# RWKV time mixing on one core: whole batches a tile, a fixed order of instructions over 512-token units, float32 stores from the sync queue

## The chip, the cores and the metric

The kernel runs on one core of a Trainium2 chip. A time is the device time of one execution in microseconds (us). Each kernel below was run four to six times, beside runs of the kernel before on the same chip; all runs were of the fast state, with a mean granted TensorE clock between 0.98 and 1.00. A ratio compares one kernel's runs with the runs of the kernel before in the same rounds; it isn't quite the ratio of the medians quoted beside it. The times of a profile are counted from the start of its span; a span is about 2 us shorter than the time.

The engines are called PE (matmuls; PEld is its weight load), DVE (VectorE), ACT (ScalarE), POOL (GpSimd) and SP (the sync queue), as the profile names them.

## The reference

```python
batch, seq_len, d_model = (16, 2048, 256)
x_prev[:, 1:, :] = x[:, :-1, :]              # the token before; zero for the first of a batch
xv = x * time_mix_v + x_prev * (1 - time_mix_v)
xr = x * time_mix_r + x_prev * (1 - time_mix_r)
v = xv @ value_weight
r = xr @ receptance_weight
out = (sigmoid(r) * v) @ output_weight       # float32; the key branch does not reach the output
```

x and out are 33.5 MB each. The kernels fold `time_mix` into the weights, so that what is left per element is `mix = c * x_prev + x` with `c = 1/time_mix - 1`, for v and for r.

## The kernel before

A tile is 1024 consecutive tokens; half of it, 512 tokens, is called a unit here. There are 64 units. The instruction order is left to the compiler's scheduler.

```python
for b in range(B):
    for it in range(NT):                                  # 2 tiles a batch
        nc.gpsimd.dma_start(out=x_bf, in_=x[b, t0:t0+T, :].rearrange("(tb p) d -> p tb d", p=P))
        # 16 transposes on PE into two PSUM tiles, then
        nc.scalar.copy(out=xt[:, :, 1:1+TH], in_=psum_xt[0])
        nc.scalar.copy(out=xt[:, :, 1+TH:1+T], in_=psum_xt[1])
        nc.vector.tensor_copy(out=xt[:, :, 0:1], in_=prev_xt[:, :, T:T+1])
        # mix: four scales of 1024 elements, two adds of 2048, all on DVE
        ...
        for h in range(2):                                # a unit
            # psum_v: 4 matmuls, psum_r: 4 matmuls (512 columns each)
            nc.scalar.activation(out=s_sb, in_=psum_r, func=ACT.Sigmoid)
            nc.vector.tensor_tensor(out=z_sb, in0=s_sb, in1=psum_v, op=ALU.mult)
            # psum_o: 8 matmuls of 256 columns on z_sb
            nc.scalar.copy(out=o_sb[:, h], in_=psum_o)    # o_sb is bf16
        nc.gpsimd.dma_start(out=out[...], in_=o_sb)       # casts to float32 on the way
```

In PSUM, the memory that matmuls write, the kernel keeps two buffers for transposes and one each for v, r and the output.

Of the kernel before, what the change touches and what calls it, by code (L numbers as in the profile page):

```python
# [1 line left out]

# [6 lines left out]
FP32 = mybir.dt.float32  # L10
BF16 = mybir.dt.bfloat16
ALU = mybir.AluOpType
ACT = mybir.ActivationFunctionType


@with_exitstack
def kernel(
    ctx: ExitStack,
    tc: tile.TileContext,
    x: bass.AP,  # L20
    time_mix_k: bass.AP,
    time_mix_v: bass.AP,
    time_mix_r: bass.AP,
    key_weight: bass.AP,
    value_weight: bass.AP,
    receptance_weight: bass.AP,
    output_weight: bass.AP,
    out: bass.AP,
):
    nc = tc.nc  # L30

    B, S, D = x.shape
    P = 128
    KO = D // P
    TH = 512
    T = 2 * TH
    HB = TH // P
    NT = S // T
    XTW = T + 8

    consts = ctx.enter_context(tc.tile_pool(name="consts", bufs=1))

    ident = consts.tile([P, P], BF16)
    make_identity(nc, ident)

    tmv_sb = consts.tile([P, KO], FP32)
    nc.sync.dma_start(out=tmv_sb, in_=time_mix_v.rearrange("(ko p) -> p ko", p=P))
    tmr_sb = consts.tile([P, KO], FP32)
    nc.sync.dma_start(out=tmr_sb, in_=time_mix_r.rearrange("(ko p) -> p ko", p=P))

    cv_sb = consts.tile([P, KO], FP32)
    nc.vector.reciprocal(cv_sb, tmv_sb)
    nc.vector.tensor_scalar(  # L53
        out=cv_sb, in0=cv_sb, scalar1=-1.0, scalar2=None, op0=ALU.add
    )
    cr_sb = consts.tile([P, KO], FP32)
    nc.vector.reciprocal(cr_sb, tmr_sb)
    nc.vector.tensor_scalar(
        out=cr_sb, in0=cr_sb, scalar1=-1.0, scalar2=None, op0=ALU.add
    )  # L60
    c_sb = [cv_sb, cr_sb]

    ones = consts.tile([P, T], BF16)
    nc.vector.memset(ones, 1.0)
    c_full = []
    for m in range(2):
        cf = consts.tile([P, KO, T], BF16, name=f"c_full{m}")
        for ko in range(KO):
            nc.scalar.mul(out=cf[:, ko, :], in_=ones, mul=c_sb[m][:, ko : ko + 1])  # L69
        c_full.append(cf)  # L70

    wv_f32 = consts.tile([P, KO, D], FP32)
    nc.sync.dma_start(out=wv_f32, in_=value_weight.rearrange("(ko p) n -> p ko n", p=P))
    wr_f32 = consts.tile([P, KO, D], FP32)
    nc.sync.dma_start(
        out=wr_f32, in_=receptance_weight.rearrange("(ko p) n -> p ko n", p=P)
    )

    wv_bf = consts.tile([P, KO, D], BF16)
    wr_bf = consts.tile([P, KO, D], BF16)  # L80
    wo_bf = consts.tile([P, KO, D], BF16)
    for ko in range(KO):
        nc.scalar.mul(out=wv_bf[:, ko, :], in_=wv_f32[:, ko, :], mul=tmv_sb[:, ko : ko + 1])
        nc.scalar.mul(out=wr_bf[:, ko, :], in_=wr_f32[:, ko, :], mul=tmr_sb[:, ko : ko + 1])
    nc.gpsimd.dma_start(out=wo_bf, in_=output_weight.rearrange("(ko p) n -> p ko n", p=P))  # L85

    xpool = ctx.enter_context(tc.tile_pool(name="xpool", bufs=4))
    xtpool = ctx.enter_context(tc.tile_pool(name="xtpool", bufs=3))
    mixpool = ctx.enter_context(tc.tile_pool(name="mixpool", bufs=3))
    zpool = ctx.enter_context(tc.tile_pool(name="zpool", bufs=4))  # L90
    opool = ctx.enter_context(tc.tile_pool(name="opool", bufs=3))
    ps_xt_pool = ctx.enter_context(tc.tile_pool(name="ps_xt", bufs=2, space=bass.MemoryType.PSUM))
    ps_vr_pool = ctx.enter_context(tc.tile_pool(name="ps_vr", bufs=1, space=bass.MemoryType.PSUM))
    ps_o_pool = ctx.enter_context(tc.tile_pool(name="ps_o", bufs=1, space=bass.MemoryType.PSUM))

    prev_xt = None
    for b in range(B):
        for it in range(NT):
            t0 = it * T

            x_bf = xpool.tile([P, 2 * HB, D], BF16, name="x_bf")
            nc.gpsimd.dma_start(  # L102
                out=x_bf,
                in_=x[b, t0 : t0 + T, :].rearrange("(tb p) d -> p tb d", p=P),
            )

            xt = xtpool.tile([P, KO, XTW], BF16, name="xt")

            psum_xt = []
            for h in range(2):  # L110
                ps = ps_xt_pool.tile([P, KO, TH], BF16, name="ps_xt")
                for tb in range(HB):
                    for ko in range(KO):
                        nc.tensor.transpose(  # L114
                            out=ps[:, ko, tb * P : (tb + 1) * P],
                            in_=x_bf[:, h * HB + tb, ko * P : (ko + 1) * P],
                            identity=ident,
                        )
                psum_xt.append(ps)
            nc.scalar.copy(out=xt[:, :, 1 : 1 + TH], in_=psum_xt[0])  # L120
            nc.scalar.copy(out=xt[:, :, 1 + TH : 1 + T], in_=psum_xt[1])  # L121

            if it == 0:
                nc.vector.memset(xt[:, :, 0:1], 0.0)
            else:
                nc.vector.tensor_copy(out=xt[:, :, 0:1], in_=prev_xt[:, :, T : T + 1])  # L126
            prev_xt = xt

            mix = mixpool.tile([P, 2, KO, T], BF16, name="mix")
            for m in range(2):  # L130
                for ko in range(KO):
                    nc.vector.tensor_scalar(  # L132
                        out=mix[:, m, ko, :],
                        in0=xt[:, ko, 0:T],
                        scalar1=c_sb[m][:, ko : ko + 1],
                        scalar2=None,
                        op0=ALU.mult,
                    )
            xwin = xt[:, :, 1 : T + 1]
            for m in range(2):  # L140
                nc.vector.tensor_tensor(  # L141
                    out=mix[:, m], in0=mix[:, m], in1=xwin, op=ALU.add
                )

            o_sb = opool.tile([P, 2, HB, D], BF16, name="o_sb")
            for h in range(2):
                psum_v = ps_vr_pool.tile([P, KO, TH], FP32, name="psum_v")
                psum_r = ps_vr_pool.tile([P, KO, TH], FP32, name="psum_r")
                for mo in range(KO):
                    for ko in range(KO):  # L150
                        nc.tensor.matmul(  # L151
                            out=psum_v[:, mo, :],
                            lhsT=wv_bf[:, ko, mo * P : (mo + 1) * P],
                            rhs=mix[:, 0, ko, h * TH : (h + 1) * TH],
                            start=(ko == 0),
                            stop=(ko == KO - 1),
                        )
                for mo in range(KO):
                    for ko in range(KO):
                        nc.tensor.matmul(  # L160
                            out=psum_r[:, mo, :],
                            lhsT=wr_bf[:, ko, mo * P : (mo + 1) * P],
                            rhs=mix[:, 1, ko, h * TH : (h + 1) * TH],
                            start=(ko == 0),
                            stop=(ko == KO - 1),
                        )

                s_sb = zpool.tile([P, KO, TH], BF16, name="s_sb")
                nc.scalar.activation(out=s_sb, in_=psum_r, func=ACT.Sigmoid)  # L169
                z_sb = zpool.tile([P, KO, TH], BF16, name="z_sb")  # L170
                nc.vector.tensor_tensor(out=z_sb, in0=s_sb, in1=psum_v, op=ALU.mult)  # L171

                psum_o = ps_o_pool.tile([P, HB, D], FP32, name="psum_o")
                for j in range(HB):
                    for ko in range(KO):
                        nc.tensor.matmul(  # L176
                            out=psum_o[:, j, :],
                            lhsT=z_sb[:, ko, j :: HB],
                            rhs=wo_bf[:, ko, :],
                            start=(ko == 0),  # L180
                            stop=(ko == KO - 1),
                        )
                nc.scalar.copy(out=o_sb[:, h], in_=psum_o)  # L183

            nc.gpsimd.dma_start(  # L185
                out=out[b, t0 : t0 + T, :].rearrange("(h p j) d -> p h j d", p=P, j=HB),
                in_=o_sb,
            )


# [28 lines left out]
```

## Time and profile before

| | before |
|---|---|
| time, median of the first three runs | 261.0 us (259.3 to 261.8) |
| span of the profiled run | 258.6 us |
| busy share PE / DVE / ACT | 81 / 79 / 74% |
| a unit in the steady part | 3.58 us |
| first v or r matmul, start of the last z | 17.5 us, 249.3 us |

### The profile page before, as it was taken

Reading aid. Unit: us, or ns where it says so; the run is one execution under the profiler, and the core shown is the slowest. Engines: PE = TensorE matmul, PEld = TensorE weight load, DVE = VectorE, ACT = ScalarE, POOL = GpSimd, SP = SyncE. Lnnn points to the kernel's source line nnn. Section 1 sums busy time; section 2 is a strip of 40 time slices with the busy share of each in tenths; the row PEclk is TensorE's granted clock in tenths of the full one; section 3 lists DMA queues with packets and bytes.
Section 4 is the critical chain, followed back from the end, with each engine's and each line's share of the span. In section 5 each row is a group of like instructions: output and inputs, shape, how many; then the busy total and the mean of one; then the engine's idle time right before and its main releaser. Section 6 shows DMA issues by size and latency. Waiting matters only on the chain.

```text
span 258.6 us, 3915 instructions
## 1 busy us (share of the span) xinstructions
PE 208.8 (81%) x1508; PEld 136.5 (53%) x1536; DVE 205.3 (79%) x293; ACT 192.0 (74%) x202; POOL 53.0 (20%) x71
## 2 busy tenths in 40 slices
PE   0288989888988889888889888988888987787860
PEld 0265655555666556565556655655555664354430
DVE  3087999888889888888888998888888899885330
ACT  6678979777777887877777788787777777645640
POOL 7031421222222211222222221112211111100111
PEclk9999999999999999999999999999999999999997
DMA  5999999999999999999999999999974343344444
GB/s 114 188 198 197 150 270 220 275 230 233 227 202 200 197 214 245 238 219 231 228 230 213 197 195 206 243 243 224 224 205 162 111 153 119 116 153 165 162 162 162
DMA packets 43362, 51.24 MB, mean 198 GB/s; under 512 B 1616, under 2 KB 35152, under 8 KB 43344
## 3 DMA queue, kind: packets, MB, share of 16 engines
q0 software_dynamic: 42256, 50.47, 89.3%
q1 hardware_dynamic: 1088, 0.53, 0.7%
q8 instruction: 12, 0.20, 0.3%
q14 instruction: 6, 0.05, 0.1%
HBM read 34.34 MB, written 33.55 MB: 263 GB/s over the span
## 4 chain that ended last, share of the span: by engine, by line
issue 67%; POOL 16%; PE 6%; DMA 4%; ACT 3%; POOLq 1%
POOL x_bf L102 8%; POOL out_dram L185 8%; DMA x_bf<-in_x_dram 4%; PE ps_xt L114 2%; PE psum_v L151 2%; PE psum_r L160 1%; PE psum_o L176 1%; ACT xt L120 1%; ACT s_sb L169 1%; ACT xt L121 1%; POOL wo_bf L85 0%; ACT o_sb L183 0%; POOLq L214 0%; POOLq L185 0%; POOLq L102 0%
## 5 line engine op out<-in xcount | busy, mean ns | idle before, releaser
L171 DVE TENSOR_TENSOR z_sb<-s_sb,psum_v 128x1024 bf16<-128x1024 bf16 x64 | 77.8, 1216 | 31.6 <-PE psum_v L151 28.3
L183 ACT CAST o_sb<-psum_o 128x1024 bf16<-128x1024 f32 x64 | 65.9, 1030 | 37.3 <-PE psum_o L176 37.3
L176 PE MATMUL psum_o<-wo_bf,z_sb 128*128 128x256 bf16 x512 | 67.3, 274 | 16.5 <-DVE z_sb L171 16.4
L169 ACT ACTIVATE s_sb<-psum_r 128x1024 bf16<-128x1024 f32 x64 | 66.0, 1032 | 17.5 <-PE psum_r L160 16.6
L141 DVE TENSOR_TENSOR mix<-mix,xt 128x2048 bf16<-128x2048 bf16 x64 | 77.7, 1218 | 0.0
L160 PE MATMUL psum_r<-mix,wr_bf 128*128 128x512 bf16 x244 | 65.2, 379 | 5.1 <-ACT s_sb L169 4.4
L176 PEld LDWEIGHTS <-z_sb 128*128 128x128 bf16 x512 | 52.1, 115 | 30.8 <-DVE z_sb L171 30.5
L151 PE MATMUL psum_v<-mix,wv_bf 128*128 128x512 bf16 x240 | 64.3, 382 | 0.7 <-issue 0.2
L114 PE MATMUL ps_xt<-ident,x_bf 128*128 128x128 bf16 x512 | 41.0, 228 | 20.5 <-DMA x_bf<-in_x_dram 12.0
L185 POOL DMA_DIRECT2D out_dram<-o_sb x32 | 22.6, 705 | 169.2 <-ACT o_sb L183 169.2
L114 PEld LDWEIGHTS <-x_bf 128*128 128x128 bf16 x512 | 35.6, 102 | 37.8 <-issue 15.4
L160 PEld LDWEIGHTS <-wr_bf 128*128 128x128 bf16 x256 | 25.1, 98 | 30.1 <-issue 0.7
L132 DVE TENSOR_SCALAR mix<-xt,cv_sb 128x1024 bf16<-128x1024 bf16 x64 | 28.7, 490 | 9.4 <-ACT xt L121 9.3
L120 ACT COPY xt<-ps_xt 128x1024 bf16<-128x1024 bf16 x32 | 32.7, 1021 | 3.7 <-PE ps_xt L114 3.7
L102 POOL DMA_DIRECT2D x_bf<-in_x_dram x32 | 29.0, 907 | 30.5 <-PE ps_xt L114 30.4
L151 PEld LDWEIGHTS <-wv_bf 128*128 128x128 bf16 x256 | 25.2, 99 | 16.1 <-issue 0.6
L121 ACT COPY xt<-ps_xt 128x1024 bf16<-128x1024 bf16 x32 | 33.1, 1034 | 0.0
L132 DVE TENSOR_SCALAR mix<-xt,cr_sb 128x1024 bf16<-128x1024 bf16 x64 | 28.5, 484 | 0.0
L126 DVE COPY xt<-xt 128x2 bf16<-128x2 bf16 x16 | 2.7, 169 | 1.2
L69 ACT ACTIVATE c_full<-ones,cv_sb 128x1024 bf16<-128x1024 bf16 x2 | 2.2, 1140 | 1.4 <-DVE cv_sb L53 1.4
L69 ACT ACTIVATE c_full<-ones,cr_sb 128x1024 bf16<-128x1024 bf16 x2 | 2.2, 1132 | 0.0
L69 ACT ACT_TABLE_LOAD x1 | 1.3, 1283 | 0.7 <-PEq L203 0.7
(16 smaller groups left out, 8.0 us busy)
## 6 DMA issues: line engine op xcount, KB each, us to landing
out_dram<-o_sb POOLq DMA_DIRECT2D x32, 1024.0 KB, 4.9
x_bf<-in_x_dram POOLq DMA_DIRECT2D x32, 512.0 KB, 7.2
wv_f<-in_value_weight_dram SPq DMA_DIRECT2D x1, 256.0 KB, 4.2
wr_f<-n_receptance_weight_dram SPq DMA_DIRECT2D x1, 256.0 KB, 4.3
wo_bf<-in_output_weight_dram POOLq DMA_DIRECT2D x1, 128.0 KB, 4.5
tmv_sb<-in_time_mix_v_dram SPq DMA_DIRECT2D x1, 1.0 KB, 2.1
tmr_sb<-in_time_mix_r_dram SPq DMA_DIRECT2D x1, 1.0 KB, 2.2
```

The lines of the kernel that those rows point to most:

```text
L102: nc.gpsimd.dma_start(out=x_bf, in_=x[b, t0 : t0 + T, :].rearrange("(tb p) d -> p tb d", p=P),)
L114: nc.tensor.transpose(out=ps[:, ko, tb * P : (tb + 1) * P], in_=x_bf[:, h * HB + tb, ko * P : (ko + 1) * P], identity=ident,)
L121: nc.scalar.copy(out=xt[:, :, 1 + TH : 1 + T], in_=psum_xt[1])
L132: nc.vector.tensor_scalar(out=mix[:, m, ko, :], in0=xt[:, ko, 0:T], scalar1=c_sb[m][:, ko : ko + 1], scalar2=None, op0=ALU.mult,)
L141: nc.vector.tensor_tensor(out=mix[:, m], in0=mix[:, m], in1=xwin, op=ALU.add)
L151: nc.tensor.matmul(out=psum_v[:, mo, :], lhsT=wv_bf[:, ko, mo * P : (mo + 1) * P], rhs=mix[:, 0, ko, h * TH : (h + 1) * TH], start=(ko == ...
L160: nc.tensor.matmul(out=psum_r[:, mo, :], lhsT=wr_bf[:, ko, mo * P : (mo + 1) * P], rhs=mix[:, 1, ko, h * TH : (h + 1) * TH], start=(ko == ...
L169: nc.scalar.activation(out=s_sb, in_=psum_r, func=ACT.Sigmoid)
L171: nc.vector.tensor_tensor(out=z_sb, in0=s_sb, in1=psum_v, op=ALU.mult)
L176: nc.tensor.matmul(out=psum_o[:, j, :], lhsT=z_sb[:, ko, j :: HB], rhs=wo_bf[:, ko, :], start=(ko == 0), stop=(ko == KO - 1),)
L183: nc.scalar.copy(out=o_sb[:, h], in_=psum_o)
L185: nc.gpsimd.dma_start(out=out[b, t0 : t0 + T, :].rearrange("(h p j) d -> p h j d", p=P, j=HB), in_=o_sb,)
```

## The change

The intent is to let PE and DVE run without waiting for each other, and to move data in long runs. Its parts:

1. **Layout.** One batch (2048 tokens) is a tile; token p*16+j lies in partition p, so that a partition's data is one run of 16 KB in HBM. After the transposes, a block of 128 columns holds the tokens of one j, and the previous token is in the block before; only block 0 needs a shifted copy of block 15, one a batch.
2. **Order.** `manual_schedule()` fixes the order of the program. For each unit PE does r, v, a group of eight transposes seven units ahead, and the output projection of the unit before.
3. **Stores.** The output tile is float32 and goes out from the sync queue, 1 MB at a time, in place of a bf16 tile cast by a GpSimd DMA.
4. **Start.** The first batch is loaded in pieces, unneeded constants are gone, and a ramp does more transposes and mix pieces a turn than the steady part.

```diff
+    ctx.enter_context(tc.manual_schedule())
-                in_=x[b, t0 : t0 + T, :].rearrange("(tb p) d -> p tb d", p=P),
+        src = x[b].rearrange("(p j) d -> p j d", p=P)
 ...
+        nc.scalar.copy(out=xt[b][:, :, c0 : c0 + TU], in_=ps)          # in transposes(g)
+        if e == UB - 1 and b > 0:
+            nc.vector.tensor_copy(
+                out=xt[b][:, :, 1:P], in_=xt[b][:, :, J * P : (J + 1) * P - 1]
+            )
 ...
+            o_sb[b] = opool.tile([P, J, D], FP32, name="o_sb")
+            nc.sync.dma_start(out=dst[:, a : a + 2 * UJ, :], in_=o_sb[b][:, a : a + 2 * UJ, :])
 ...
+    for g in range(NU):
+        ps_r = project(g, 0, ps_r_pool, "psum_r")
+        nc.scalar.activation(out=s_sb, in_=ps_r, func=ACT.Sigmoid)
+        ps_v = project(g, 1, ps_v_pool, "psum_v")
+        took = take_pieces(g + 3, 1 if g > 8 else 2)      # mix pieces: (half batch, v or r)
+        for piece in took:
+            mixing_scale(*piece)
+        nc.vector.tensor_tensor(out=z_sb, in0=s_sb, in1=ps_v, op=ALU.mult)
+        for piece in took:
+            mixing_add(*piece)
+        advance(START_T[g] if g < len(START_T) else g + LOOK)   # START_T = [3, 4, 7, 9], LOOK = 7
+        if z_prev is not None:
+            output(g - 1, z_prev)
+        z_prev = z_sb
+    output(NU - 1, z_prev)
```

## The prediction

> **What bounds the kernel now.** I read the page first (busy shares, slices, costliest groups), then the list of waits, then one stretch of the timeline in the steady part, last the table of stretches. The shares:
>
> ```profile
> PE 208.8 (81%) x1508; PEld 136.5 (53%) x1536; DVE 205.3 (79%) x293; ACT 192.0 (74%) x202; POOL 53.0 (20%) x71
> ...
> PE   0288989888988889888889888988888987787860
> DMA  5999999999999999999999999999974343344444
> ```
>
> Three engines stand at 74 to 81%, none is full, and no slice of PE stays at 9: this is a kernel bound by waits between nearly balanced engines. The DMA row at 9 looks like a bound and has to be ruled out. The list of waits does that, as the only waits of PE for a transfer are three at the start:
>
> ```profile
> PEld L176 <- DVE z_sb L171: 30.5, 38, 1.9
> DVE z_sb L171 <- PE psum_v L151: 28.3, 29, 2.1
> PE psum_o L176 <- DVE z_sb L171: 16.4, 33, 1.4
> PE ps_xt L114 <- DMA x_bf<-in_x_dram: 12.0, 3, 10.4
> PE ps_xt L114 <- ACT xt L120: 8.1, 24, 0.5
> ```
>
> The first and third lines are one loop: PE's output projection waits for VectorE's product z, and z waits (second line) for PE's v projection of the same 512 tokens. Each engine waits for the other in turn. The timeline of one tile (1024 tokens, two units of 512) shows it:
>
> ```profile
> 63.31 1.22 DVE L171 TENSOR_TENSOR z_sb<-s_sb,psum_v 128x1024 bf16<-128x1024 bf16 x1 [0.82 <-PE psum_v L151]
> 64.36 0.44 PE L114 MATMUL ps_xt<-ident,x_bf 128*128 128x128 bf16 x5 [0.29 <-ACT xt L120]
> 64.64 1.04 PE L176 MATMUL psum_o<-wo_bf,z_sb 128*128 128x256 bf16 x8
> 65.51 0.38 PE L151 MATMUL psum_v<-mix,wv_bf 128*128 128x512 bf16 x1
> ...
> 67.37 0.70 POOL L185 DMA_DIRECT2D out_dram<-o_sb  x1 [4.90 <-ACT o_sb L183]
> 68.44 1.06 PE L176 MATMUL psum_o<-wo_bf,z_sb 128*128 128x256 bf16 x8 [0.43 <-DVE z_sb L171]
> ...
> 74.52 0.71 POOL L185 DMA_DIRECT2D out_dram<-o_sb  x1 [5.30 <-ACT o_sb L183]
> ```
>
> The two stores lie 7.15 us apart: that is a tile, so 3.58 us a unit. In brackets are the waits: 0.82 us of VectorE and 0.43 plus 0.29 of PE in each tile.
>
> **What the Trainium skill says.** "TensorE: Matmul & The Clock Gate", Back-to-back issue gap, gives about 216 ns for an isolated 512-column matmul and about 81 ns for a 128-column one with its weight load. The trace: four projection matmuls from 64.64 plus 0.87 to the next group, 0.87/4 = 217 ns, which agrees; a transpose with its load took about 68 ns (16 loads in 1.09 us), a little less than the page. "VectorE: DVE Perf Modes", The perf-mode tier table: a two-tensor operation reaches 2x at most on bf16 in SBUF and 1x with a PSUM operand. The trace agrees: 1218 ns for 2048 elements, the same 1216 ns for 1024 with PSUM. Neither shape is changed. "SBUF — State Buffer", Who interferes with whom: VectorE in a two-port mode and GpSimd block one another, and GpSimd writes the descriptors of its own DMAs. It shows once here: a scale pair that began at 30.99 took 1.19 us instead of 0.88 beside a load issue at 30.85 that took 1.10 instead of 0.90. "DMA: Bandwidth & Descriptors", Issuing engines are not separate DMA queues: moving the stores to the sync queue saves only issue time. No run here shows that yet.
>
> **The change part by part.**
>
> Removed: the unused constant tiles (4 ScalarE operations, 2.19 + 2.17 us at the start), the descriptor work of 32 stores on GpSimd (22.6 us, off the path), half of its load issues (32 to 16, plus the pieces of the first batch).
>
> Not removed: the arithmetic of a unit. I take the distance from start to start in back-to-back stretches, which is the real cost of an instruction in a full engine.
> - PE: r 0.87, v 0.87, output 0.87 (64.64 to 65.51), eight transposes 8 x 0.068 = 0.55. Sum 3.16 us.
> - VectorE: z 1.13 (67.17 to 68.30), add 1.13, two scales 0.80 (65.24 to 66.04 for the pair). Sum 3.06. Added: one shift copy of 2x127 elements per batch; the two-element copy took 0.17, I estimate 0.3 us, over four units 0.08. Sum 3.14.
> - ScalarE: sigmoid, transposed x, output at about 0.92 from start to start. Sum 2.8. Float32 instead of bf16 output shouldn't matter: the cast and the bf16 copy cost the same now (1030 and 1021 ns).
>
> Moved: the order. Output of unit g-1 is issued after the v projection of g, so PE no longer waits for a z in progress; transposes run seven units ahead; mix is made at least one unit ahead. With r(g) starting at 0: r results at 1.03, v at 1.90, transposes end 2.4, output 3.35. Sigmoid starts 1.12 to 1.22 and ends by 2.25; z starts 2.31, ends 3.52. The next v needs z's PSUM banks at 3.16 + 0.87 = 4.03, so 0.5 us are spare. VectorE after z: add at 3.45, scales at 4.58, free at 5.38; the next z is due at 2.31 + 3.16 = 5.47, spare 0.09. ScalarE's output copy starts at 3.45 and leaves the next sigmoid at most 0.1 late. So the loop closes at PE's 3.16 us, and VectorE (3.14) is nearly the same. Steady gain: 3.58 - 3.16 = 0.42 us a unit.
>
> Start: now the first tile's load lands at 10.44, the first v matmul begins at 17.46. Changed: the first 4-row piece is 0.5 MB instead of 1 MB. Successive tiles landed at 10.44, 13.14 and 15.78, so about 1 MB of float32 per 2.65 us, 0.4 MB/us. Half a megabyte less is 1.3 us, and it leads the queue: I estimate 7 us. Cold transposes 0.9, ScalarE copy 1.0, four half-size scales 1.1, one half-size add 0.7: first r matmul at about 11. The ramp is not free. Units 2 to 5 need their mix before VectorE has caught up, and up to unit 6 PE does 13 groups of transposes and VectorE 9 pieces of mix; stepping the orders of both through by hand gives r(6) at 35 us instead of 11 + 6 x 3.16 = 30. Some of it is work done early (about six groups of transposes, 3.3 us), the rest is stall.
>
> Rest: from r(6), 58 units x 2.61 = 151.4, and 51 groups of transposes x 0.55 = 28.0, sum 179.4, so PE ends its work at 35.2 + 179.4 = 214.6. VectorE from 37.2: 58 z x 1.13 = 65.5, 55 pieces x 1.93 = 106.2, copies 4: 213. Last z that PE must wait for 0.7, result 0.2, half copies 0.7, store 3.5 (256 KB loads on this queue took 4.2 and 4.3; it is 256 KB pieces here too): 219.7 us of span. Between the median time and the span lie 261.0 - 258.6 = 2.4 us. That makes 222. I add 2 us for jitter of two engines that have no more than 0.1 us of slack each: 224 us, 0.86 of before.
>
> **The rivals.**
> 1. The DMA becomes the bound. For: its row is at 9 while loads and stores overlap, 0.47 with stores alone (159 GB/s in the stretch from 190 to 210). A store of 1 MB thus costs 0.47 x 6.6 = 3.1 us of all engines, a load at most 2.65 (the landings above). A batch is 2 MB each way: 11.5 us, against 4 x 3.16 = 12.6 us of compute. Full to 91%, so it should fit, and 8 to 16 KB runs should be no slower than 1 KB ones. Against it as well: the loads have two batches' lead. If mixing reads and writes at 332 GB/s (2 x 0.524 MB in 3.16 us) is not to be had and the rate stays at the present 293 (2 x 1.05 MB in 7.16), a unit stays at 3.58 us and the time ends at some 245.
> 2. VectorE becomes the bound through the fixed order: if z is late behind the scale pieces, v is late, and each late turn adds up. If each unit loses 0.2 us in this loop, 64 x 0.2 = 13 us: 235. For: spare 0.09 us only. Against: v has 0.5 us to give.
> 3. ScalarE: three 1 us operations in 3.16 us. A sigmoid queued behind an output copy delays z. I counted 0.1 us; 0.3 would make it 64 x 0.3 minus the slack, some 230.
> 4. Better than thought: start at 9, no ramp stall, transposes at 0.45: 216.
>
> **Range and chances.** From the sum 222 without jitter down to rival 4 gives the lower end 216; rivals 2 and 3 set the upper end 236. Rival 1 in full has perhaps one chance in twelve and would still be faster by 6%. A change that is no faster needs a wait I do not see: 4% for the same, 1% for slower.
>
> **What would show it.** Right: a steady distance of about 3.16 us from one sigmoid to the next; PE at 90% or more in the middle slices; the waits of the output projection for z and of z for v nearly gone; loads never waited for after the start; the first r matmul near 11 us, r(6) near 35; the DMA row at about 8 or 9 for the whole span. Wrong: transposes that wait for x (rival 1), v matmuls that wait for z (rival 2), z that waits for the sigmoid (rival 3), a store tail over 5 us, scale or add durations that differ from 0.44 and 1.22 us, a granted clock under 0.99.

## More of the kernel before

One more view is worth a look, because it misleads: the chain of work that ended last, by engine, for the kernel before.

```profile
issue 67%; POOL 16%; PE 6%; DMA 4%; ACT 3%; POOLq 1%
```

The chain ends in the last store, follows GpSimd's queue of loads and stores back through the whole run, and calls two thirds of it time in which nothing was waited for. It doesn't name the loop between PE and DVE at all. The list of waits does.

## The result and the profile after

The changed kernel takes 229.47 us (median of four, 228.24 to 229.76), ratio 0.879 with a 95% interval of 0.875 to 0.883: 12% faster. Predicted were 224 us and a range of 216 to 236.

Busy shares and slices of the changed kernel (each digit is a fortieth of the span, in tenths):

```profile
PE 201.8 (89%) x1510; PEld 129.8 (57%) x1538; DVE 203.4 (89%) x288; ACT 185.4 (81%) x194; POOL 13.8 (6%) x41
...
PE   0294879899999999999999999999999999989881
...
DVE  2478299999999999999999999999999999999941
...
DMA  5969999999999898989999898989897444434364
```

DVE is at 9 in every slice from the sixth to the last but two, and PE nearly so. Both do the same arithmetic as before: DVE's busy time fell only from 205.3 to 203.4 us and PE's from 208.8 to 201.8. What went is the idle time. The busy columns of the stretch from 60 to 180 us say it most plainly (PE, PEld, DVE, ACT, POOL, clock, DMA share, GB/s). First the kernel before:

```profile
60.00:180.00 120.00, 106.65 (x794) 70.51 (x807) 105.68 (x152) 95.24 (x101) 27.33 (x34) 1.00 1.01 221
```

Then the changed kernel:

```profile
60.00:180.00 120.00, 117.04 (x899) 76.38 (x914) 118.93 (x164) 109.24 (x116) 5.85 (x19) 1.00 0.91 253
```

DVE went from 105.7 to 118.9 us of 120. The remaining 1.1 us are gaps of some 0.1 us around the shift copies. So VectorE is the bound now, and PE has some slack. The list of waits (total us, times, longest) has lost the loop:

```profile
PE psum_v L176 <- DVE z_sb L295: 4.5, 17, 0.6
PE ps_t L128 <- DMA x_bf<-in_x_dram: 2.9, 1, 2.9
DVE z_sb L295 <- PE psum_v L176: 2.8, 1, 2.8
PEld L192 <- DVE z_sb L295: 1.0, 1, 1.0
```

Before, the output projection waited for z for 16.4 us (30.5 for its weight loads) and z for v 28.3; now it is 1.0 and one wait of 2.8, in the ramp. The 17 waits of v for z are new. Thirteen of them (3.0 us, the longest 0.5) lie between 36 and 200 us, after shift copies: DVE is late, and PE waits. The other four (1.5 us) lie in the last units, where PE has no transposes left to do. The timeline from a place of the first kind:

```profile
112.15 1.21 DVE L295 TENSOR_TENSOR z_sb<-s_sb,psum_v 128x1024 bf16<-128x1024 bf16 x1
112.54 1.03 PE L176 MATMUL psum_r<-mix,w_bf 128*128 128x512 bf16 x4
113.28 1.22 DVE L161 TENSOR_TENSOR mix<-mix,xt 128x2048 bf16<-128x2048 bf16 x1
...
114.42 0.22 DVE L136 COPY xt<-xt 128x254 bf16<-128x254 bf16 x1
...
114.75 0.89 DVE L152 TENSOR_SCALAR mix<-xt,c_sb 128x1024 bf16<-128x1024 bf16 x2
115.55 1.21 DVE L295 TENSOR_TENSOR z_sb<-s_sb,psum_v 128x1024 bf16<-128x1024 bf16 x1
...
116.81 1.02 PE L176 MATMUL psum_v<-mix,w_bf 128*128 128x512 bf16 x4 [0.19 <-DVE z_sb L295]
...
124.72 1.21 DVE L295 TENSOR_TENSOR z_sb<-s_sb,psum_v 128x1024 bf16<-128x1024 bf16 x1
```

Read DVE's column: each instruction starts where the one before ends. From z at 112.15 to z four units later at 124.72 are 12.57 us, 3.14 us a unit; the shift copy takes 114.42 to 114.75 of it, 0.33 us a batch.

The chain that ended last now names the bound:

```profile
DVE 73%; issue 12%; PE 6%; DMA 3%; POOL 2%; ACT 2%; POOLq 0%; DVEq 0%
```

### The profile page after: what moved, and what is told of

The parts are those of the page before. It is cut to its first block, busy times and chain, and to the rows that moved or that the text cites. A ratio compares the mean times of both kernels' runs of the same rounds, so it can differ in the third digit from the quotient of the medians.

```text
span 227.6 us, 3894 instructions
## 1 busy us (share of the span) xinstructions
PE 201.8 (89%) x1510; PEld 129.8 (57%) x1538; DVE 203.4 (89%) x288; ACT 185.4 (81%) x194; POOL 13.8 (6%) x41
## 4 chain that ended last, share of the span: by engine, by line
DVE 73%; issue 12%; PE 6%; DMA 3%; POOL 2%; ACT 2%; POOLq 0%; DVEq 0%
DVE mix L161 29%; DVE z_sb L295 29%; DVE mix L152 14%; DMA x_bf<-in_x_dram 3%; PE psum_o L192 2%; PE psum_v L176 2%; PE psum_r L176 1%; ACT xt L134 1%; DVE xt L136 1%; POOL x_bf L80 1%; POOL xt L124 1%; POOL wo_bf L118 1%; PE ps_t L128 0%; ACT o_sb L210 0%; DVE o_sb L207 0%
## 5 line engine op out<-in xcount | busy, mean ns | idle before, releaser
L176 PEld LDWEIGHTS <-w_bf 128*128 128x128 bf16 x512 | 50.3, 99 | 58.3 <-issue 12.4
L161 DVE TENSOR_TENSOR mix<-mix,xt 128x2048 bf16<-128x2048 bf16 (+1 forms) x66 | 77.8, 1186 | 0.0
L134 ACT COPY xt<-ps_t 128x1024 bf16<-128x1024 bf16 x60 | 60.4, 1013 | 19.0 <-PE ps_t L128 18.9
L210 ACT COPY o_sb<-psum_o 128x1024 f32<-128x1024 f32 x63 | 64.2, 1019 | 6.9 <-PE psum_o L192 6.8
L176 PE MATMUL psum_v<-mix,w_bf 128*128 128x512 bf16 x243 | 64.9, 383 | 5.3 <-DVE z_sb L295 4.5
L176 PE MATMUL psum_r<-mix,w_bf 128*128 128x512 bf16 x241 | 65.4, 388 | 1.6 <-DVE mix L161 1.2
L152 DVE TENSOR_SCALAR mix<-xt,c_sb 128x1024 bf16<-128x1024 bf16 (+1 forms) x132 | 56.4, 473 | 3.5 <-ACT xt L238 1.8
L192 PEld LDWEIGHTS <-z_sb 128*128 128x128 bf16 x512 | 47.8, 98 | 7.3 <-DVE z_sb L295 1.0
L128 PE MATMUL ps_t<-ident,x_bf 128*128 128x128 bf16 x480 | 36.1, 219 | 3.9 <-DMA x_bf<-in_x_dram 2.9
L72 POOL DMA_DIRECT2D x_bf<-in_x_dram x16 | 8.7, 544 | 121.6 <-PE ps_t L128 118.2
L238 ACT COPY xt<-ps_t 128x1024 bf16<-128x1024 bf16 x4 | 4.0, 1014 | 9.2 <-PE ps_t L232 9.2
L232 PE MATMUL ps_t<-ident,x_bf 128*128 128x128 bf16 x32 | 3.1, 265 | 5.7 <-DMA x_bf<-in_x_dram 5.7
L145 PE MATMUL ps_t<-ident,x_bf 128*128 128x128 bf16 x2 | 0.4, 298 | 3.8 <-DMA x_bf<-in_x_dram 3.8
## 6 DMA issues: line engine op xcount, KB each, us to landing
x_bf<-in_x_dram POOLq DMA_DIRECT2D x15, 1024.0 KB, 10.2
```

The source lines that it names most:

```text
L72: nc.gpsimd.dma_start(out=x_bf[b][:, lo:hi, :], in_=src[:, lo:hi, :])
L128: nc.tensor.transpose(out=ps[:, ko, jj * P : (jj + 1) * P], in_=x_bf[b][:, e * UJ + jj, ko * P : (ko + 1) * P], identity=ident,)
L134: nc.scalar.copy(out=xt[b][:, :, c0 : c0 + TU], in_=ps)
L152: nc.vector.tensor_scalar(out=mix[b][:, m, ko, lo:hi], in0=xt[b][:, ko, lo:hi], scalar1=c_sb[:, m, ko : ko + 1], scalar2=None, op0=ALU.mult,)
L161: nc.vector.tensor_tensor(out=mix[b][:, m, :, lo:hi], in0=mix[b][:, m, :, lo:hi], in1=xt[b][:, :, lo + P : hi + P], op=ALU.add,)
L176: nc.tensor.matmul(out=ps[:, mo, :], lhsT=w_bf[:, m, ko, mo * P : (mo + 1) * P], rhs=mix[b][:, m, ko, e * TU : (e + 1) * TU], start=(ko == 0),
```

## The experiments

Eleven edited kernels and one control ran. Those whose name begins with b are edits of the kernel before, those with a of the changed kernel. All results were correct but those of two. Their outputs are wrong, which doesn't matter for the times.

| kernel | time, us | ratio to before | last z starts, us | span, us |
|---|---|---|---|---|
| before | 260.1 to 260.7 | 1 | 249.3 | 258.6 |
| changed | 229.47 | 0.879 | 220.5 | 227.6 |
| changed again, the control of the last set | 229.17 | 0.880 | 219.4 | 226.5 |
| b1: before, fixed order, short lead | 244.65 | 0.941 | 233.1 | 242.9 |
| b3: before, fixed order, full lead | 232.42 | 0.893 | 220.4 | 230.2 |
| a1: output without the lag | 299.24 | 1.150 | 290.7 | 297.4 |
| a2: stores of before | 232.10 | 0.892 | 219.8 | 230.0 |
| a6: loads in 1 KB runs | 230.70 | 0.886 | 222.6 | 229.6 |
| a3: scheduler's order | 235.27 | 0.903 | 226.7 | 233.8 |
| a4: second load issued earlier | 229.32 | 0.883 | 218.3 | 225.3 |
| a5: one scale for two | 222.00 | 0.854 | 213.0 | 220.1 |
| a7: a scale done twice | 261.64 | 1.007 | 252.4 | 259.4 |
| a9: shift copy on ACT | 224.30 | 0.862 | 216.2 | 223.2 |
| a8: a9, a4 and an earlier ramp | 220.68 | 0.848 | 211.9 | 219.0 |

### Is it the order, or the layout and the transfers?

The theory of the prediction was that the order carries the gain. The rival was that the long runs and the sync queue do. The kernel before was given the order alone: its 1024-token tiles, 1 KB loads, two-element copies, bf16 stores by GpSimd and its own start stay.

```diff
+    ctx.enter_context(tc.manual_schedule())
     for n in range(NTT):
         for h in range(2):
-            # v, r, sigmoid, z, output of the same unit, in the scheduler's order
+            psum_r = project(n, h, 1, wr_bf, "psum_r")          # r first, then sigmoid, then v
+            psum_v = project(n, h, 0, wv_bf, "psum_v")
+            scale(n + 1, 1 - h)                                 # a mix piece of the next tile
+            nc.vector.tensor_tensor(out=z_sb, in0=s_sb, in1=psum_v, op=ALU.mult)
+            add(n + 1, 1 - h)
+            transposes(n + 2, h)
+            output(*z_prev)                                     # one unit late
```

> The kernel before with the fixed order alone: r, v, eight transposes two tiles ahead, output one unit late, mix of the next tile in two pieces; its own token layout, 1 KB loads, bf16 stores with a cast by GpSimd and its own start are kept. Theory (the gain is the order): VectorE has 3.06 us a unit here plus a two-element copy, so units of 3.1 to 3.2 us; the start stays near 17 to 18 us; about 64 x 0.4 = 26 us less than before, 233 to 238 us, ratio 0.90. Rival (layout and transfers carry the gain): stays above 250 us.

It took 244.65 us: between the two expectations, so neither theory as stated. Its waits tell why:

```profile
PE psum_v L151 <- DVE mix L143: 9.6, 16, 1.2
PE psum_v L151 <- DVE xt L125: 8.7, 15, 0.9
```

In every second unit PE waits some 0.56 us for the mix of v. I had made that piece in the unit directly before, behind z on DVE, so PE caught up with it. (The second line names the small column write that DVE does right after the add.) Two units took 127.07 - 120.24 = 6.83 us. The second variant makes each piece one unit earlier and runs the transposes six halves ahead:

```diff
-            scale(n + 1, 1 - h) ... add(n + 1, 1 - h) ... transposes(n + 2, h)
+        took = (2, 3) if u == 0 else (u + 3,)                   # u counts units; piece q is (tile q // 2, r or v)
+        advance((5, 7)[u] if u < 2 else u + 6)                  # transposes up to this half tile
```

> As the first variant of the kernel before in the fixed order, but each piece of mix is made one unit earlier and the transposes run six halves ahead; layout, loads and stores of before are kept. The first variant made half of its v projections wait for a mix piece of the unit just before (0.56 us each). Theory (the order with enough lead is the gain): VectorE full at about 3.13 us a unit, 242.9 - 32 x 0.55 = 225 to 231 us of span, within 1.5% of the changed kernel. Rival (old transfers or layout cost something in the steady part): stays at 240 us with VectorE idle.

232.42 us, ratio 0.893. The stretch from 60 to 180 us of this kernel:

```profile
60.00:180.00 120.00, 116.34 (x884) 77.98 (x899) 119.25 (x170) 107.56 (x114) 31.24 (x38) 1.00 1.14 248
```

DVE is as full as in the changed kernel (119.3 against 118.9 of 120), with the old transfers, and the last z starts at 220.4 us against 220.5. So the order with enough lead brings 260.3 - 232.4 = 27.9 us of the 260.1 - 229.2 = 30.9 us in all. What is left, some 3 us, lies behind the last z, where the stores are: 230.2 - 220.4 = 9.8 us there, 227.6 - 220.5 = 7.1 us in the changed kernel.

The two reach that z by different ways, which the full DVE hides. In b3 z of unit 6 (counted from 0) starts at 40.16 us, in the changed kernel at 43.20; after it a batch takes b3 12.78 us and the changed kernel 12.57. Nearly all of that difference is the two-element copy, which in b3 runs beside the issue of a store on GpSimd and takes twice what it took before (0.35 us, the median of 16, in place of 0.17):

```profile
106.01 0.71 POOL L176 DMA_DIRECT2D out_dram<-o_sb  x1 [4.27 <-ACT o_sb L174]
106.34 0.34 DVE L127 COPY xt<-xt 128x2 bf16<-128x2 bf16 x1
```

### What do the stores and the runs bring by themselves?

a2 puts the stores of before back into the changed kernel, a6 makes the loads short.

```diff
-            o_sb[b] = opool.tile([P, J, D], FP32, name="o_sb")      # a2
+            o_sb[b] = opool.tile([P, J, D], BF16, name="o_sb")
-            nc.sync.dma_start(out=dst[...], in_=o_sb[b][...])       # a2, all three places
+            nc.gpsimd.dma_start(out=dst[...], in_=o_sb[b][...])
-    src = x[b].rearrange("(p j) d -> p j d", p=P)                   # a6, wrong result on purpose
+    src = x[b].rearrange("(j p) d -> p j d", p=P)
```

> The changed kernel with the stores of before: bf16 tile, cast in a GpSimd DMA. Theory: transfers are hidden and the cast on ScalarE costs the same, so 229 to 231 us (within 1%). Rival: VectorE is now full, so descriptor writing that blocks its scales costs directly: 32 stores x 0.3 us = 10 us, 238 us.

> The changed kernel whose loads take tokens j*128+p, so runs of 1 KB instead of 16 KB (the result is wrong on purpose, the work is the same). Theory: loads are two batches ahead and land in time; only the start may lose, 229 to 232 us. Rival 1 of the prediction: transfers near their limit, short runs make loads late after the start and the time goes above 235 us with transposes waiting for x.

a2 took 232.1 us, a little more than the theory's 231 and far from the rival's 238. The same stretch of a2:

```profile
60.00:180.00 120.00, 118.06 (x917) 76.41 (x916) 118.93 (x163) 109.17 (x115) 19.75 (x38) 1.00 0.88 253
```

DVE's 118.93 us are those of the changed kernel to the digit, and they hold as many instructions (163 and 164), although GpSimd is busy 19.75 us in place of 5.85 with the issue of DMAs. The steady part loses nothing; the last z starts at 219.8 us, between the 219.4 and 220.5 of the changed kernel's two profiles. The loss is at the end: 230.0 - 219.8 = 10.2 us behind the last z against 7.1. I first put this down to a longer landing of the stores, and the trace refutes it: the last 256 KB stores land 2.3 us after their issue where they took 2.1. In both kernels the last output copy ends 4.07 us behind the start of the last z.

a2 moves its last bytes just before 226.0 and ends 4.0 us later; the changed kernel moves its last ones before 226.5 and ends little more than 1 us later. So the 3 us are the close of the program after the last byte. The timeline leaves the closing instructions out, but `prof LABEL --source` with the line of the last one lists them (count, shortest/median/longest in ns, first and last start in us). First a2, then the changed kernel:

```profile
L328 POOLq DRAIN  x3: 45/93/5034, 224.2 to 229.7; - x3
L328 POOLq DRAIN  x3: 45/102/1754, 190.0 to 227.3; - x3
```

In a2 GpSimd's closing DRAIN starts with its last store's issue, at 224.2, and takes 5.03 us; the span ends 0.8 us after it. In the changed kernel GpSimd's last DMA is a load, its DRAIN is over at 191.8, and the span ends 0.9 us after the last store has landed. All fourteen profiles go one way or the other: the four with stores from GpSimd (before, b1, b3, a2) have a DRAIN of 4.95 to 5.03 us there, behind stores of 1 MB and of 256 KB alike, and end 5.7 to 5.8 us after the issue of the last store, the ten others 2.9 to 3.0 us after it. That difference is the 3 us. Why the DRAIN takes 5 us the traces don't show.

a6 took 230.7 us, in the theory's range. Its DMA share from 60 to 180 us is 1.12 in place of 0.91, and no transpose waited for x after the start. It is 1 to 2 us slower because z of the first unit started at 17.5 us in place of 15.4. So the long runs brought nothing in the steady part.

### What does the lag bring, and what the fixed schedule?

```diff
-        if z_prev is not None:                                  # a1
-            output(g - 1, z_prev)
-        z_prev = z_sb
-    output(NU - 1, z_prev)
+        output(g, z_sb)
-    ctx.enter_context(tc.manual_schedule())                     # a3
```

> The changed kernel, but the output projection is issued in its own unit, right after z and the transposes. Theory: PE now waits for z each time; v ends, z takes 1.33 us, the transposes hide 0.45 of it, so units of 3.06 + 0.9 = about 3.9 us and some 265 to 275 us, slower than the kernel before. Rival (the lag matters little, the lead of the transposes and of mix is what counts): under 240 us.

> The changed kernel without the fixed schedule: the same program, the instruction order left to the compiler's scheduler. Its listed order has the same lag, but splits some transposes and puts the mix adds ahead of z at places. Theory: the lag of the output and the lead of the transposes are kept by the scheduler in most units, so 229 to 236 us. If z is pushed behind whole mix pieces, v waits, and it comes to 240 or more.

a1 took 299.2 us: slower as expected, but by 24 to 34 us more than the theory said. The chain is longer than I counted. One round of it in a1's timeline:

```profile
121.60 1.22 DVE L295 TENSOR_TENSOR z_sb<-s_sb,psum_v 128x1024 bf16<-128x1024 bf16 x1 [1.19 <-ACT s_sb L284]
...
122.88 1.05 PE L192 MATMUL psum_o<-wo_bf,z_sb 128*128 128x256 bf16 x8 [1.11 <-DVE z_sb L295]
...
123.97 1.02 ACT L210 COPY o_sb<-psum_o 128x1024 f32<-128x1024 f32 x1 [1.15 <-PE psum_o L192]
...
124.88 1.03 ACT L284 ACTIVATE s_sb<-psum_r 128x1024 bf16<-128x1024 f32 x1
...
125.94 1.22 DVE L295 TENSOR_TENSOR z_sb<-s_sb,psum_v 128x1024 bf16<-128x1024 bf16 x1 [0.85 <-ACT s_sb L284]
```

z, output, output copy, sigmoid of the next unit, next z: a ring of 4.34 us (121.60 to 125.94). I had left out ScalarE: its order is output copy, then sigmoid, so a late output delays the next unit's sigmoid, and with it z.

a3 took 235.27 us, in the range of the theory. The scheduler keeps the lag, and DVE's busy time from 60 to 180 us is 118.99. Of the 6 us 3.6 are lost in the ramp, where the first z starts at 18.5 us in place of 15.4 and one z waits 6.0 us for v: z of unit 6 starts at 46.78 us in place of 43.20. The other 2.7 are lost after it (179.93 us to the last z in place of 177.26), which DVE's full busy time doesn't show.

### Is VectorE's sum the bound?

If it is, what is added to DVE must show in full, and what is taken from it must show until PE's own 3.06 us bind.

```diff
-        for ko in range(KO):                                    # a7: a scale twice
+        for ko in (0, 0, 1):
-        for ko in range(KO): tensor_scalar(1024 elements)       # a5: one scale of 2048, wrong on purpose
+        tensor_scalar(2048 elements, one constant)
-            nc.vector.tensor_copy(out=xt[b][:, :, 1:P], ...)    # a9: the shift copy on ACT
+            nc.scalar.copy(out=xt[b][:, :, 1:P], ...)
```

> The changed kernel with one of the two scales of each piece done twice: 0.40 us more of VectorE a unit, nothing else. Theory (VectorE full): nearly all of it shows, 60 x 0.4 = 24 us: 252 to 254 us. Rival (slack in VectorE): less than 15 us.

> The changed kernel with one scale of 2048 elements in place of two of 1024 (wrong result on purpose: one constant for both halves). It takes 0.15 to 0.2 us of VectorE out of each unit and leaves all else. Theory (VectorE at 3.14 us a unit is the bound, PE next at 3.06): PE takes over after 0.08 us, 58 x 0.08 = 4 to 5 us less, 224 to 226 us. Rival (the loop between engines, not VectorE's sum, sets the pace): no change, 229 us.

> The changed kernel with the shift copy, once a batch, on ScalarE instead of VectorE. It takes 0.33 us from start to start out of VectorE in every fourth unit, and puts about 0.4 us on ScalarE, which has some 0.3 us free a unit. Theory (VectorE's sum is the pace): four units take 12.25 instead of 12.57 us until PE's 4 x 3.06 = 12.24 binds; 15 x 0.32 = 4.8 us less, 224 to 226 us. Rival (ScalarE's delay of the output copy and of the sigmoid gives it back): 228 us or more.

a7 took 261.64 us, 32.5 more than the control, where the theory said 24. Its timeline has the reason:

```profile
140.71 1.40 DVE L152 TENSOR_SCALAR mix<-xt,c_sb 128x1024 bf16<-128x1024 bf16 x3
142.02 1.21 DVE L295 TENSOR_TENSOR z_sb<-s_sb,psum_v 128x1024 bf16<-128x1024 bf16 x1
```

Three scales take 142.02 - 140.71 = 1.31 us from start to start, where two took 0.80: the repeat costs 0.51, not 0.40, and 64 x 0.51 = 32.6 us is the whole difference. (The repeat starts 0.04 us after the scale before it has ended, while the third starts before the second has ended. The repeat overwrites what the scale just wrote, so it may have to wait for that write; this is my reading, no run takes the two apart.) Nothing of the added work was hidden.

a5 took 222.0 us, 7 less than the changed kernel where 4 to 5 were expected. In the steady part z follows z by 2.93 to 3.28 us, r follows r by 3.05, and PE's groups leave no gap (119.05 us busy of 120): PE took over. From z of unit 6 to the last z are 171.86 us in place of 177.26 in the control, 5.4 us less; another 1.0 lies before it (41.16 in place of 42.17). The medians are 7.2 us apart, these two profiles 6.4.

a9 took 224.30 us, as the theory said, and is correct. That 0.33 us in every fourth unit are worth 4.9 us (4.4 of them between z of unit 6 and the last z, 172.90 in place of 177.26) shows how tightly DVE was loaded. ScalarE had the room.

### The ramp, and a faster version

In the first 40 us the changed kernel lost time. Lines of its timeline:

```profile
11.73 1.91 PE L176 MATMUL psum_r<-mix,w_bf 128*128 128x512 bf16 x4
...
20.44 0.62 PE L128 MATMUL ps_t<-ident,x_bf 128*128 128x128 bf16 x8 [2.94 <-DMA x_bf<-in_x_dram]
...
21.99 1.91 PE L176 MATMUL psum_r<-mix,w_bf 128*128 128x512 bf16 x4
...
25.45 1.22 DVE L295 TENSOR_TENSOR z_sb<-s_sb,psum_v 128x1024 bf16<-128x1024 bf16 x1 [2.84 <-PE psum_v L176]
...
28.70 0.23 DVE L136 COPY xt<-xt 128x254 bf16<-128x254 bf16 x1 [2.03 <-ACT xt L134]
```

The transposes of unit 4 need the second batch, whose load was issued at 12.6 us: GpSimd's queue holds the cast of the output weights before it, and that waited until 11.4 us for its data. PE stood idle for 2.94 us, and from 21.5 to 24.9 us its granted clock was 0.50: four matmuls of r took 1.91 us, and v followed 1.71 us after r, where 0.87 is the rule. DVE waited 2.84 us for that v, and then 2.03 us for transposes of unit 7, without which the shift copy of the second batch can't run.

The control is the same kernel, and its profile shows how much of this is the clock. The stretch from 20.4 to 25.0 us, first of the changed kernel, then of the control (the third number from the end is the granted clock):

```profile
20.40:25.00 4.60, 4.56 (x24) 2.45 (x25) 2.21 (x2) 3.05 (x3) 0.00 (x0) 0.63 1.03 215
20.40:25.00 4.60, 4.26 (x40) 2.71 (x41) 3.40 (x4) 3.16 (x4) 0.00 (x0) 1.00 1.04 217
```

In the control PE waited 1.98 us for the second batch and stayed at full clock. DVE still waited 1.20 us for v of unit 2 and 2.03 us for the shift copy, and r of unit 6 began at 38.82 us in place of 39.86. So the half rate comes and goes from run to run: of the ten runs of this kernel, the six with a mean clock of 0.988 to 0.990 took 229.3 to 230.5 us, the four with 0.995 or 0.996 took 228.1 to 228.8.

a4 moves only the load. a8 has also the shift copy on ACT, and issues the transposes of units 4 to 7 in one turn.

```diff
+    load(1, [(0, J)])                          # a4, a8: before the wait for the output weights
     nc.gpsimd.tensor_copy(out=wo_bf, in_=wo_f32)
-    START_T = [3, 4, 7, 9]                     # a8
+    START_T = [3, 7, 8, 9]
```

> The changed kernel, but GpSimd issues the load of the second batch before it waits for the output weights. Theory (4.7 us of my miss lie in the ramp, and part of it is this load, issued at 12.6 us and landed at 20.4): the transposes of unit 4 start near 17 us, VectorE's 2.8 us wait for v of unit 2 mostly goes, 1.5 to 3 us less: 226.5 to 228 us. Rival (the ramp is bound by VectorE's own pieces): less than 0.5 us.

> The changed kernel unaltered, as the control of this set's rounds: 228 to 230 us. If it spreads by 3 us, as the run with the earlier load did, then the start is what varies from run to run.

> Shift copy on ScalarE, the second batch's load issued before the wait for the output weights, and transposes of units 4 to 7 all issued in the second turn of the ramp. Theory: 4.8 us from the shift copy as above, and 2 to 4 of the ramp's 7.6 us of idle VectorE: 221 to 223.5 us, the fastest correct version. Rival (PE in order blocks on the second batch's load instead, and the ramp costs the same): 225 us.

a4 can't be decided by its times: 227.07 in the profiled run and 229.3 to 230.2 in the four others, ratio 0.8825 (0.878 to 0.887), where the control has 0.8803 (0.876 to 0.885) and spreads by 2.4 us itself. The profile of its fastest run shows the step: the transposes of unit 4 at 17.68 us in place of 20.44, z of the third unit at 23.25 in place of 25.45. One of these 2.2 us is the clock, as the control has 24.42. The gain isn't there in every run, and DVE's waits of 1.20 and 2.03 us are in a4 as in the control: they don't come from the load.

a8 took 220.68 us (six runs, 220.49 to 221.26), ratio 0.848: 3.7% faster than the changed kernel, correct, and it hardly spreads; its six runs have clocks of 0.993 to 0.997, so none seems to have had the half rate. DVE does not wait between z of the second unit and z of the fifth but for 0.1 us, and PE's clock from 20 to 25 us is 1.00, as in the control. Its steady stretch:

```profile
60.00:180.00 120.00, 120.00 (x946) 78.84 (x943) 120.00 (x159) 114.73 (x128) 6.99 (x18) 1.00 0.90 253
```

PE and DVE are both full. Of the 8.5 us that a8 gains over the control, a9 accounts for 4.9; 3.6 belong to the two changes of the ramp together. These are medians over runs with and without the half rate. The profiles of a8 and of the control, both at full clock, are 7.5 us apart at the last z: 3.2 up to z of unit 6 and 4.3 after it.

## Why the prediction was right, point by point

**The mechanism was right.** The waits in a ring between PE and DVE were the bound, and the order takes them away: b3 shows 27.9 of the 30.9 us with nothing else changed. That transfers were hidden, against the DMA row at 9, was right as well: a2 and a6 have the same steady part with the old stores and with short loads (3.15 and 3.14 us a unit, the changed kernel 3.15). Float32 output costs ScalarE nothing (1019 ns a copy, before 1030). That the sync queue saves only issue time, as the prediction cites, holds in the steady part and not at the end, where a2 loses 3 us.

**The steady unit was right in size, with two terms the other way round.** The prediction had PE at 3.16 us and DVE at 3.14, and so named PE as the pace. Measured are 3.06 and 3.14. The term that was off is the group of transposes: 0.55 us predicted, 0.44 measured (111.22 to 111.66 in the changed kernel). I had taken 68 ns from a group in the kernel before, reading it from PEld's row (its "16 loads in 1.09 us" stands in no line of the trace as such; near the lines shown are 11 loads in 0.82 and 4 in 0.26); but the weight loads of a group span longer than the group's share of PE (0.65 us for eight in the changed kernel, of which PE's next group waits for only 0.44). DVE's sum was right to the digit, the estimate of 0.3 us for the shift copy too (0.33). So VectorE is the bound, through its own sum and not through the late-z loop of rival 2: a7, a5 and a9 show it from three sides. Of the signs of being wrong, three showed: v waiting for z (4.5 us in all), z waiting for the sigmoid (2.9 us, in the last two units), and a mean clock of 0.988 in one run.

**The step that was mis-sized is the ramp.** The sum had r of unit 6 at 35.2 us. It began at 39.86, 4.7 us late. The first r was where I put it (11.73 for 11). In my stepping I had the second batch land in time and PE at full rate. The load was issued behind a wait that I hadn't followed in GpSimd's order, and PE's half rate after idling, stated by the Trainium skill, "TensorE: Matmul & The Clock Gate", Why this matters for your kernels (no idle gaps over some 3 us between bursts of matmuls, else half clock), was not in the sum. The traces agree in kind, but with a shorter gap than the page's. Once the clock had risen, a wait of PE of 2.13 us or more (2.94 in the changed kernel, 2.67 in a9, 2.76 and 2.21 in a7, 2.13 in a6, 3.79 in a3) always came with a stretch at half the clock, one of 1.98 us or less (control) never; at half the clock a matmul of 512 columns takes 0.43 us.

These two are only half of the miss. At full clock r of unit 6 begins at 38.82 us (control), with the earlier load too at 37.66 (a4), with the transposes of units 4 to 7 in one turn and the shift copy on ACT as well at 35.93 (a8), against 35.2 in the sum. So the clock is 1.0 of the 4.7 us, the load 1.2, the order of the ramp 1.7, and 0.7 stay open; each step rests on one profile of each kernel.

**The rest was a little short too.** From r of unit 6 to the end of the span 187.7 us were measured and 184.5 in the sum. The sum gave the units after the last transposes PE's own 2.61 us, but VectorE still had mix to make there and set the pace: from r of unit 57 to r of unit 63 are 17.78 us where the sum had 15.66, 2.1 more. Another 1.6 lie behind that last r (9.3 and 7.7), and the units before gave back 0.5. The span is 1.9 us below the time instead of 2.4, which had compared a median with another run's span; in every run the two are 1.7 to 2.2 apart. 4.7 + 3.2 - 0.5 = 7.4, which is what separates the sum of 222 from 229.5; the 2 us of jitter in the prediction covered part of it, by luck, as none of these terms is jitter but for the clock.

**Where the earlier start went.** The changed kernel's first r is 4.3 us earlier than b3's (11.7 and 16.0), yet their last z's start at the same time. The ramp gave back more than the start, as z of unit 6 starts 3.0 us later than b3's, and the shorter batches made these 3 us up. That wasn't in the prediction, and a8 gets some 3.5 us of the ramp back.

## What to carry to other kernels

When PE and a vector engine wait for each other in turn although each is only 80% busy, a lag of one unit between a product and its consumer, together with enough lead for everything else that they exchange, takes the waits away; b1 shows that too short a lead gives little more than half of the gain (15.8 of 27.9 us). After that, count the fullest engine's instructions from start to start: small copies that nobody minded before then cost what they take, and may be worth moving to an engine with room. A busy share near 100% doesn't end the search: b3 and a3 have DVE busy for 119.3 and 119.0 of 120 us, no less than the changed kernel, and still need 3.20 and 3.21 us a unit where it needs 3.15. A DMA row at 9 says nothing of a bound as long as no engine waits for a transfer, and an earlier first instruction is worth nothing if the ramp behind it stalls.

## What the Trainium skill lacked or had wrong

- "TensorE: Matmul & The Clock Gate", Back-to-back issue gap, gives about 81 ns for a 128-column matmul with its load and about 131 ns for one of 512 columns in a stream, and calls 56 and 216 ns the figures of isolated ones. In the changed kernel eight transposes took 0.44 us from the first to the next group's start, 55 ns each with their loads, and four 512-column matmuls 0.87 us, 217 ns each: both run in streams and take the figures for isolated ones. Part 4: PE-mode transpose, gives about 275 ns as the duration of one transpose in a kernel; here it is 219 ns, the mean of 480.
- "SBUF — State Buffer", Who interferes with whom, says that GpSimd and a VectorE instruction in a two-port mode block each other. It doesn't say how much that costs a full VectorE, and here it depends on what meets. In b3 the two-element copy beside a store's issue took 0.35 us in place of 0.17. In a2, with 35 stores issued from GpSimd, VectorE's scales took 481 ns as without them, while the load issues that ran beside the shift copy and the scales took 0.74 us in place of 0.53, so there the delay may have fallen on GpSimd.
- No page has what stores from GpSimd cost at the end of a program: its closing DRAIN took 4.95 to 5.03 us from its last store's issue (before, b1, b3, a2), and the span ended 5.7 to 5.8 us after that issue, against 2.9 to 3.0 with stores from the sync queue.
- "VectorE: DVE Perf Modes", The DRAIN you can't avoid, says a semaphore after each copy costs nothing extra. A scale that overwrote the output of the scale before it added 0.51 us, where its neighbour took 0.40; the page has no such case.
